# Two block products and a bank copy of an output projection given out ahead of the last gate of the input projection

## The chip, the cores and the metric

One core of a Trainium2 chip runs the kernel. The metric is the device time of one execution in microseconds (us); the median of several runs counts. In the profile, PE is TensorE (matmul), PEld its weight load, DVE is VectorE, ACT is ScalarE, POOL is GpSimd and SP is SyncE, which issues most of the DMAs.

## The reference

One layer of a decoder trunk on a sequence of 1024 tokens and 1024 channels, all in float32:

```
h = rms_norm(x, g_mix)
z = h @ w_in + b_in
va, ga, xb, gb, sa, sb = split(z)            # 1024, 1024, 1536, 1536, 1024, 1024 columns
u   = silu(layer_norm(causal_conv31(va * sigmoid(ga)), ln_g, ln_b))
y_a = u @ w_a_out                            # stage "ga"
v   = rg_lru(causal_conv4(xb))
y_b = (v * gelu(gb)) @ w_b_out               # the stage that is changed
m   = sigmoid(sa) * y_a + sigmoid(sb) * y_b
x   = x + m @ w_o
x   = x + relu(rms_norm(x, g_mlp) @ w_1) ** 2 @ w_2
out = rms_norm(x, g_final)
```

## The kernel before

Every float32 operand is held as two parts in a shorter format, a high part (a ScalarE copy, names ending in `h`) and the low rest (a VectorE subtraction, `l`). A product of two blocks takes three matmuls: high by high, high by low, low by high. Matmuls are 128 x 128 by 128 x 512. Tokens are split into even and odd ones, or into two halves of 512. Larger products are formed from seven products of half blocks instead of eight, with sums of blocks as operands.

The stages follow one another, and TensorE's work is laid out by hand as a list of steps. Two of them matter here:

- **The input projection**, `zseq`. Each step `(i, p)` is one block product of 12 matmuls into a PSUM bank. `z_post` and `z_post2` take the results out one and two steps later: gates go through a sigmoid on ScalarE (tile `zg`, line 937) and are stored to DRAM (`gates`). Two more rounds, `n = L` and `n = L + 1`, follow behind the last step; they take out the last results and prepare operands. The table `ZX` says which loads and splits are given out at which step: `hg_parts(t)` splits tile `t` of the gated recurrence output for the next stage.
- **The product with w_b_out**, `bseq`. For four pairs of output blocks (`i` = 0 to 3), its steps are `"1"` to `"7"` with 6 matmuls each (block products on the four tiles of the recurrence output that go through the seven products, operands `hb1` to `hb7` from `hb_parts` and `hb_t`) and `"00"`, `"01"`, `"10"`, `"11"` with 24 matmuls each (plain products on the other eight tiles, operands `hg0` to `hg9`). `b_mm` gives out the matmuls of a step, `b_post` what follows them at the next step. Results are shared between banks by copies on ScalarE (line 1161): `"1"` is copied from bank b to a, `"7"` from f to an SBUF tile, `"6"` from b to e, `"5"` from e to g. Only then may further matmuls be added to the source bank. The eight banks of PSUM are handed out in turn.

The table `BX` gives the loads and splits for each step of `bseq`: `p_load` and `p_parts` the plain weights (`wbp`), `a_load`, `a_sums` and `a_parts` the weights of the seven products (`wba`, `wbs`), `b_gate` the stored gates (`sb`), `n_load` and `n_ahead` the convolution's output for the layer norm (`q`, `yc`).

Beside these steps runs the layer norm of `u`, a generator `n_all`: statistics of the odd tokens and of the even tokens (`n_stats`: the mean by matmuls with a matrix of ones, eight differences and squares, the variance by matmuls again, a root), then scaling with Silu of the even (`n_scale(0)`) and of the odd tokens (`n_scale(1)`). Where it yields `"pause"`, nothing more of it is given out in this step. `n_to(k)` drives it on until `k` pieces are scaled.

The order on each engine is the order in which this program gives instructions out. What VectorE has to do in a step is first collected by `later` with a time at which it is ready, then sorted by that time in `vector_work`; gaps are filled with pieces of `n_all` according to the planner's own clocks `clk`, which count estimated costs for TensorE, ScalarE and VectorE. ScalarE, VectorE and SP each work through their list in order.

Of the kernel before, what the change touches and what calls it, by code (L numbers as in the profile page):

```python
# [9 lines left out]
F32 = mybir.dt.float32  # L10
# [3 lines left out]
ALU = mybir.AluOpType  # L14
# [16 lines left out]
def trunk_kernel(ctx: ExitStack, tc: tile.TileContext, x, xt_in, xt_eo, vecs, w_in, w_a_out, w_b_pl, w_b_sq,  # L31
# [948 lines left out]
    with tc.manual_schedule(engines=ENGINES):  # L980
# [60 lines left out]
        def p_parts(j):  # L1041
            if j < 8:
                wop[j, "p"] = b_split(wraw_.pop((j, "p")), f"wbp{j}", W if j else T)

        L = len(zseq)
        ZX.update({L - 16: ((a_load, 0),), L - 13: ((a_sums, 0), (hb_load, 0, 0)),
                   L - 12: ((a_parts, 0, "a"), (hb_load, 0, 1)), L - 11: ((a_parts, 0, "s"), (hb_load, 1, 1)),
# [2 lines left out]
                   L - 6: ((hb_parts, 6), (hg_load, 2)), L - 5: ((p_parts, 0), (hg_load, 3, 6)),  # L1050
                   L - 4: ((hg_parts, 0), (hg_load, 7)), L - 3: ((hg_parts, 1), (hg_load, 8)),
                   L - 2: ((hg_parts, 2, 3), (hg_load, 9)), L - 1: ((hb_parts, 2), (hg_parts, 6)),
                   L: ((hg_parts, 7, 8),), L + 1: ((hg_parts, 9),)})
        for n in range(6):
            z_get(n, z_sums)
        vector_work(clk["V"])
# [37 lines left out]
    def W(name, dt=F32):  # L1094
        return wp.tile([P, S], dt, tag="w", name=name)

    def bank(name):
        return zp.tile([P, HS], F32, tag="z", name=name)

    def low(l, src, h):  # L1100
        tt(l, src, h.bitcast(F32), ALU.subtract)  # L1101

    PLAIN = (0, 1, 2, 3, 6, 7, 8, 9)
    bseq = [(0, "1")]
    for i in range(4):
        bseq += [(i, x) for x in ("7", "6", "00", "5", "2", "4", "01", "3", "10")]
        bseq += [(i + 1, "1")] * (i < 3) + [(i, "11")]
    sb, yb_, fs = {}, {}, {}

    def b_gate(j):  # L1110
        for hf in range(2):
            sb[j, hf] = EV(f"sb{j}{hf}").rearrange("p (o n) -> p o n", o=2)
            nc.sync.dma_start(sb[j, hf], halved(spill[1, j], hf))

    def b_mm(i, x):
        if len(x) == 1:
            p = int(x)
            b = {1: "b", 2: "a", 3: "e", 4: "b", 5: "e", 6: "b", 7: "f"}[p]
            if p in (1, 7):
                yb_[i, b] = bank(f"yb{i}{b}")  # L1120
            (h, l), k0 = wop[i, "a" if p in (1, 2, 4) else "s"], \
                {1: 0, 2: 1, 4: 3, 5: 0, 6: 1, 7: 2, 3: 3}[p]
            vh, vl = hbo[p]
            if i == 3:
                del hbo[p]
            ops = [(h[:, c:c + P], l[:, c:c + P], vh[:, hs], vl[:, hs])
                   for c, hs in ((2 * P * k0, HALVES[0]), (2 * P * k0 + P, HALVES[1]))]
            if p in (3, 4):
                del wop[i, "s" if p == 3 else "a"]
            new = p in (1, 7)  # L1130
        else:
            m_, hf = int(x[0]), int(x[1])
            b, new = {"00": "a", "01": "e", "10": "b", "11": "g"}[x], False
            h, l = wop[2 * i + m_, "p"]
            ops = [(h[:, n * P:(n + 1) * P], l[:, n * P:(n + 1) * P], *(a[:, HALVES[hf]] for a in hg[t]))
                   for n, t in enumerate(PLAIN)]
            if hf:
                del wop[2 * i + m_, "p"]
        todo = [y for w, wl, h, l in ops for y in ((w, h), (w, l), (wl, h))]
        for n, (w, v) in enumerate(todo):  # L1140
            nc.tensor.matmul(yb_[i, b], w, v, start=new and n == 0, stop=n == len(todo) - 1,  # L1141
                             skip_group_check=not new)
        at("P", len(todo) * MM)

    def b_out(i, m_, hf, src):
        j = 2 * i + m_
        g = sb.pop((j, hf))

        def mult():
            tt(g, src.rearrange("p (n o) -> p o n", o=2), g, ALU.mult)  # L1150
            nc.sync.dma_start(halved(mbd[j], hf), g)

        later(0, 0.69, mult)

    def b_post(i, x):
        def copy(to, b):
            if to == "f":
                t = fs[i] = EV(f"ybf{i}")
            else:
                t = yb_[i, to] = bank(f"yb{i}{to}")  # L1160
            nc.scalar.activation(t, yb_.pop((i, b)) if to == "f" else yb_[i, b], AF.Copy)
            at("A", 0.62)

        if x in ("1", "7", "6", "5"):
            copy(*{"1": "ab", "7": "ff", "6": "eb", "5": "ge"}[x])
        elif x in ("2", "3"):
            b_out(i, 0, int(x == "3"), yb_.pop((i, "a" if x == "2" else "e")))
        elif x == "10":
            c = EV(f"ybc{i}")
            later(0, 0.69, tt, c, yb_.pop((i, "b")), fs[i], ALU.add)  # L1170
            b_out(i, 1, 0, c)
        elif x == "11":
            c = fs.pop(i)
            later(0, 0.69, tt, c, yb_.pop((i, "g")), c, ALU.add)
            b_out(i, 1, 1, c)


    q, mean, vacc, rstd, nsum, nspl = {}, {}, {}, {}, {}, {}

# [35 lines left out]
    def n_stats(o):  # L1215
        held = []

        def add(s):
            if o in vacc:
                tt(vacc[o], vacc[o], s, ALU.add)  # L1220
                v_at()
            else:
                vacc[o] = s

        n_split(ysum[0][:, HALVES[o]], f"mu{o}")
        yield "pause"
        mean[o] = n_mm(f"mu{o}")
        yield "pause"
        for n, (kk, c2, i) in enumerate(PIECES8):
            if o:  # L1230
                n_ahead(1)
                a = ahead.pop(0)
            else:
                a = q[kk, o, c2][:, HALVES[i]]
            tt(a, a, mean[o], ALU.subtract)
            v_at()
            if o:
                nc.sync.dma_start(yd[4 * kk + 2 * c2 + i, :, HALVES[1]], a)
            s = EV(f"sq{o}{n}")
            nc.scalar.activation(s, a, AF.Square)  # L1240
            at("A", 0.62, clk["V"])
            if held:
                add(held.pop(0))
            held.append(s)
            yield True
        add(held.pop(0))
        mean.pop(o)
        n_split(vacc.pop(o), f"var{o}")
        yield "pause"
        pv = n_mm(f"var{o}")  # L1250
# [25 lines left out]
    def n_all():  # L1276
        yield from n_stats(1)
        while (0, 0, 0) not in q:
            yield "pause"
        yield from n_stats(0)  # L1280
        ysum.clear()
        yield from n_scale(0)
        while (0, 1, 0) not in q:
            yield "pause"
        yield from n_scale(1)

    norm = n_all()

    scaled = [0]
# [466 lines left out]
        7: ((g_parts, "u", 5, 1), (up_lhs, 1, 5), (g_t, "u", 0, 3), (g_t, "u", 1, 3))}.items()})  # L1756
    BX = {}
    for i in range(4):
        BX.update({(i, "7"): ((b_gate, 2 * i), (p_parts, 2 * i + 1), (a_load, i + 1))[::1 if i else 2],
                   (i, "6"): ((p_load, 2 * i + 2),), (i, "5"): ((a_sums, i + 1),),  # L1760
                   (i, "01"): ((a_parts, i + 1, "a"), (b_gate, 2 * i + 1)),
                   (i, "10"): ((a_parts, i + 1, "s"), (p_parts, 2 * i + 2), (p_load, 2 * i + 3))})
    for k, v in {(0, "1"): ((p_load, 1), (hb_parts, 5)), (0, "7"): ((hb_t, 4),), (0, "6"): ((hb_parts, 4),),
                 (0, "00"): ((hb_parts, 3),), (0, "2"): ((p_parts, 1), (n_ahead, 6)), (0, "10"): ((n_load, 0),),
                 (2, "11"): ((n_load, 1),),
                 (3, "00"): ((g_load, "a", 0, 0), (g_load, "a", 1, 0)),
                 (3, "4"): ((n_to, 4), (g_parts, "a", 1, 0), (g_parts, "a", 1, 1)),
                 (3, "01"): ((g_load, "a", 2, 0), (g_load, "a", 3, 0), (g_get, 0, g_lhs), (g_get, 1, g_lhs)),
                 (3, "3"): ((n_to, 16), (g_t, "a", 0, 1, 2), (g_t, "a", 1, 1, 2), (g_get, 2, g_lhs),
                           (g_get, 3, g_lhs)),  # L1770
                 (3, "10"): ((g_load, "a", 0, 1),),
                 (3, "11"): ((g_parts, "a", 2, 0), (g_parts, "a", 2, 1), (g_load, "a", 1, 1))}.items():
# [413 lines left out]
```

## Time and profile before

| | |
|---|---|
| time, median of 3 runs | 1552.56 us (1552.04 to 1553.2) |
| the profiled execution: its own time | 1549.72 us |
| its span | 1548.0 us |
| granted TensorE clock, mean over the span | 0.998 |
| first matmul of `bseq` | 628.72 us from the span's start |
| first matmul of `ga`, the stage behind it | 765.78 us |

In the profile, a row of a timeline has the start in us from the span's start, the duration, the engine, the line, the operation and `written<-read`. In brackets behind it stands how long the engine had been idle just before it, and what released it. A row of the windows has the stretch, its length and the busy time of PE, PEld, DVE, ACT and POOL with instruction counts, then the granted TensorE clock, the DMA share and GB/s.

### The profile page before, as it was taken

How to read it: one execution, taken by the hardware profiler on the slowest of the kernel's cores; microseconds unless marked ns; L12 is line 12 of the kernel's file. 1: busy time of each engine (PE TensorE's matmuls, PEld its weight loads, DVE VectorE, ACT ScalarE, POOL GpSimd, SP SyncE). 2: the span in 40 equal slices, each digit the busy share in tenths (PEclk: the TensorE clock that was granted, in tenths of full speed). 3: DMA queues.
4: the chain of work that ended last, by engine and by line, in shares of the span. 5: the costliest groups of instructions: out<-in, count | busy, mean ns of one | idle time of the engine just before them, and what ended most of it. 6: DMA issues, size and time to landing. Idle time of an engine off the chain costs nothing.

```text
span 1548.0 us, 19213 instructions
## 1 busy us (share of the span) xinstructions
PE 1530.0 (99%) x6758; PEld 1258.2 (81%) x6758; DVE 1247.2 (81%) x1679; ACT 917.4 (59%) x1280; POOL 184.4 (12%) x219
## 2 busy tenths in 40 slices
PE   9999999999999999899999999999999999999998
PEld 7888788888888888788788888888888888888886
DVE  6899999979899998687779879755555558888897
ACT  6648576567667567544575777554444475555553
POOL 0000000002222222000022332000000001111110
PEclk9999999999999999999999999999999999999999
DMA  8776978898997779863779898333333779888862
GB/s 345 196 188 161 250 189 223 217 275 219 251 245 200 184 193 275 271 205 116 240 210 300 195 195 214 137 121 113 114 115 110 242 210 228 220 224 223 209 129 109
DMA packets 134593, 312.03 MB, mean 202 GB/s; under 512 B 13488, under 2 KB 35504, under 8 KB 134496
## 3 DMA queue, kind: packets, MB, share of 16 engines
q1 hardware_dynamic: 104048, 234.79, 46.7%
q0 software_dynamic: 30304, 75.74, 26.7%
q8 instruction: 53, 0.87, 0.2%
q14 instruction: 44, 0.36, 0.1%
q10 hardware_dynamic: 144, 0.26, 0.0%
HBM read 149.79 MB, written 60.82 MB: 136 GB/s over the span
## 4 chain that ended last, share of the span: by engine, by line
PE 89%; issue 4%; DMA 2%; DVE 1%; POOL 1%; ACT 1%; SPq 0%; POOLq 0%; ACTq 0%; DVEq 0%
PE z L726 18%; PE d L1948 15%; PE e L2068 3%; PE keep L1948 2%; PE z L258 1%; PE rg L536 1%; PE rg L534 1%; PE rg L535 1%; DMA x<-in_x_dram 1%; PE yb0b L1141 1%; ACT q L1270 1%; POOL go L66 1%; PE yb3e L1141 1%; PE yb1b L1141 1%; PE yb0e L1141 1%
## 5 line engine op out<-in xcount | busy, mean ns | idle before, releaser
L726 PE MATMUL z<-xh,win_h 128*128 128x512 f32 x400 | 125.0, 391 | 0.0
L726 PE MATMUL z<-xl,win_h 128*128 128x512 f32 x400 | 124.6, 390 | 0.0
L1960 DVE TENSOR_TENSOR acc<-acc,d 128x1024 f32<-128x1024 f32 x72 | 87.9, 1220 | 33.4 <-PE d L1948 32.7
L726 PE MATMUL z<-xh,win_l 128*128 128x512 f32 x400 | 98.3, 391 | 0.0
L726 PEld LDWEIGHTS z<-xh,win_l 128*128 128x128 f32 x400 | 75.2, 188 | 16.8
L726 PEld LDWEIGHTS z<-xh,win_h 128*128 128x128 f32 x400 | 75.0, 188 | 16.7 <-ACT win_h L67 0.7
L637 DVE SCALAR_TENSOR_TENSOR y<-u,vec,y 128x511 f32<-128x511 f32 (+14 forms) x120 | 88.5, 738 | 0.0
L726 PEld LDWEIGHTS z<-xl,win_h 128*128 128x128 f32 x400 | 75.1, 188 | 15.8
L542 ACT ACTIVATE g<-rg,vec 96x1024 f32<-96x1024 f32 x32 | 35.6, 1113 | 85.1 <-issue 46.0
L637 DVE SCALAR_TENSOR_TENSOR y<-yt,csum,y 128x511 f32<-128x511 f32 (+6 forms) x112 | 82.7, 738 | 0.0
L637 DVE SCALAR_TENSOR_TENSOR yt<-u,vec,yt 128x511 f32<-128x511 f32 (+6 forms) x112 | 82.7, 738 | 0.0
L1645 ACT ACTIVATE o<-s 128x512 fp32r<-128x512 f32 x56 | 33.7, 622 | 45.6 <-DVE s L1629 26.4
L66 POOL DMA_DIRECT2D win_l<-win_raw x25 | 21.8, 871 | 324.6 <-ACT win_l L65 294.8
L66 POOL DMA_DIRECT2D zo<-zw x42 | 36.6, 871 | 128.2 <-ACT zo L65 116.6
L486 DVE SCALAR_TENSOR_TENSOR v<-xb,vec,v 128x1023 f32<-128x1023 f32 (+2 forms) x36 | 46.2, 1283 | 7.0 <-ACT v L477 6.0
L66 POOL DMA_DIRECT2D db_1l<-wr x7 | 6.1, 869 | 310.2 <-ACT db_1l L65 287.6
L65 ACT ACTIVATE zo<-zw 128x512 fp32r<-128x512 f32 x42 | 26.3, 626 | 20.8 <-PE z10f L914 2.1
L1101 DVE TENSOR_TENSOR o<-s,o 128x512 fp32r<-128x512 f32 x56 | 37.3, 683 | 1.5 <-ACT o L1645 1.4
L66 POOL DMA_DIRECT2D zo<-zs x28 | 24.5, 873 | 76.2 <-ACT zo L65 70.9
L578 DVE TENSOR_TENSOR_SCAN g<-a,g 128x1024 f32<-128x1024 f32 x12 | 27.5, 2292 | 0.4
L66 POOL DMA_DIRECT2D ga<-gsa x8 | 7.0, 871 | 170.4 <-ACT ga L65 168.3
L67 ACT ACTIVATE win_h<-win_raw 128x1024 fp32r<-128x1024 f32 x25 | 26.2, 1046 | 0.0
(2825 smaller groups left out, 4854.2 us busy)
## 6 DMA issues: line engine op xcount, KB each, us to landing
w_raw<-in_w_dram SPq DMA_DIRECT2D x34, 512.0 KB, 5.4
fr<-fd SPq DMA_DIRECT2D x32, 512.0 KB, 5.3
wr<-in_w_dram SPq DMA_DIRECT2D x32, 512.0 KB, 6.1
zw<-in_w_in_dram SPq DMA_DIRECT2D x28, 512.0 KB, 5.6
win_raw<-in_w_in_dram SPq DMA_DIRECT2D x25, 512.0 KB, 7.0
win_l<-win_raw POOLq DMA_DIRECT2D x25, 512.0 KB, 6.6
zo<-zw POOLq DMA_DIRECT2D x42, 256.0 KB, 5.7
gates<-zg SPq DMA_DIRECT2D x32, 256.0 KB, 4.0
```

The source lines that it names most:

```text
L66: nc.gpsimd.dma_start(l, src, accum_op=ALU.add)
L486: nc.vector.scalar_tensor_tensor(v[:, d:S], a[:, 0:S - d], cbw_c[:, w * 12 + t:w * 12 + t + 1], v[:, d:S], ALU.mult, ALU.add)
L542: nc.scalar.activation(a, gps.pop((n, gi))[:HD, :], AF.Sigmoid, bias=(ba_c, bx_c)[gi][:, n:n + 1])
L578: nc.vector.tensor_tensor_scan(i, a, i, 0.0, ALU.mult, ALU.add)
L637: nc.vector.scalar_tensor_tensor(o[:, k:], a[:, 0:HS - k], c, o[:, k:], ALU.mult, add)
L726: nc.tensor.matmul(zps[s][:, HALVES[hf]], w[:, k, :], xw[k][part][hf], start=n == 0, stop=n == 23)
L1101: tt(l, src, h.bitcast(F32), ALU.subtract)
L1141: nc.tensor.matmul(yb_[i, b], w, v, start=new and n == 0, stop=n == len(todo) - 1, skip_group_check=not new)
L1645: nc.scalar.activation(o[:, 0], src, AF.Copy)
L1948: nc.tensor.matmul(o, a, b, start=n == 0 and (p != 1 or g == 0), stop=n == len(todo) - 1, skip_group_check=p == 1 and g > 0)
L1960: tt(acc[p, q2], acc[p, q2], ps, ALU.add)
L2068: nc.tensor.matmul(o, a, b, start=n == 0 and t not in LOADED, stop=n == len(todo) - 1, skip_group_check=t in LOADED)
```

## The change

- The helpers `bank`, `b_gate`, `b_mm`, `b_out` and `b_post` move ahead of the loop of the input projection, unchanged but for two calls spelled out.
- In round `L`, behind hg7, the steps (0,"1") and (0,"7") of `bseq` are given out. In round `L + 1` the copy of (0,"1") from bank b to bank a is given out ahead of the last gate's sigmoid; hg8 moves from round `L` to `L + 1`, hg9 to step (0,"6"). The loop over `bseq` starts with its third step, (0,"6").
- `BX` of the first steps: the first load of plain weights (`p_load` 1), the first gates (`b_gate` 0), `a_load` 1, hg9, hb5 and `hb_t` 4 all belong to (0,"6") now; hb4 to (0,"00") and hb3 to (0,"5"), one step later each.
- `n_stats` pauses once more between the split of a sum (mean and variance) and its matmuls.
- `n_scale(1)`, the odd tokens, starts at step (3,"5") instead of as soon as their load has been given out.

```diff
@@ ahead of the loop of the input projection: bank, bseq, b_gate, b_mm, b_out, b_post moved here @@
-                   L: ((hg_parts, 7, 8),), L + 1: ((hg_parts, 9),)})
+                   L: ((hg_parts, 7), (b_mm, 0, "1"), (b_mm, 0, "7")),
+                   L + 1: ((b_post, 0, "1"), (hg_parts, 8))})
...
@@ n_stats @@
         n_split(ysum[0][:, HALVES[o]], f"mu{o}")
         yield "pause"
+        yield "pause"
         mean[o] = n_mm(f"mu{o}")
...
         n_split(vacc.pop(o), f"var{o}")
         yield "pause"
+        yield "pause"
         pv = n_mm(f"var{o}")
...
@@ n_all @@
         yield from n_scale(0)
-        while (0, 1, 0) not in q:
+        while not landed:
             yield "pause"
         yield from n_scale(1)
 
+    landed = []
...
     for i in range(4):
-        BX.update({(i, "7"): ((b_gate, 2 * i), (p_parts, 2 * i + 1), (a_load, i + 1))[::1 if i else 2],
+        BX.update({(i, "7"): ((b_gate, 2 * i), (p_parts, 2 * i + 1), (a_load, i + 1)),
...
-    for k, v in {(0, "1"): ((p_load, 1), (hb_parts, 5)), (0, "7"): ((hb_t, 4),), (0, "6"): ((hb_parts, 4),),
-                 (0, "00"): ((hb_parts, 3),), (0, "2"): ((p_parts, 1), (n_ahead, 6)), (0, "10"): ((n_load, 0),),
+    BX[0, "6"] = (p_load, 1), (b_gate, 0), (a_load, 1), (hg_parts, 9), (hb_parts, 5), (hb_t, 4), (p_load, 2)
+    for k, v in {(0, "00"): ((hb_parts, 4),), (0, "5"): ((hb_parts, 3),), (0, "2"): ((p_parts, 1), (n_ahead, 6)),
+                 (0, "10"): ((n_load, 0),),
                  (2, "11"): ((n_load, 1),),
...
-                 (3, "4"): ((n_to, 4), (g_parts, "a", 1, 0), (g_parts, "a", 1, 1)),
+                 (3, "5"): ((landed.append, 1),), (3, "4"): ((n_to, 4), (g_parts, "a", 1, 0), (g_parts, "a", 1, 1)),
...
-        for n, step in enumerate(bseq):
+        for n, step in enumerate(bseq[2:], 2):
             taps["paused"] = False
             clk["A"], clk["V"] = max(clk["A"], clk["P"] + 0.5), max(clk["V"], clk["P"] - 2)
-            if n:
-                b_post(*bseq[n - 1])
+            b_post(*bseq[n - 1])
             b_mm(*step)
```

More of the change, by code (lines that the diff above doesn't have):

```diff
@@ L1043, in p_parts, with bank, b_gate @@
                 wop[j, "p"] = b_split(wraw_.pop((j, "p")), f"wbp{j}", W if j else T)
+        def bank(name):
+            return zp.tile([P, HS], F32, tag="z", name=name)
+        PLAIN = (0, 1, 2, 3, 6, 7, 8, 9)
+        bseq = [(0, "1")]
+        for i in range(4):
+            bseq += [(i, x) for x in ("7", "6", "00", "5", "2", "4", "01", "3", "10")]
+            bseq += [(i + 1, "1")] * (i < 3) + [(i, "11")]
+        sb, yb_, fs = {}, {}, {}
+        def b_gate(j):
+            for hf in range(2):
+                sb[j, hf] = EV(f"sb{j}{hf}").rearrange("p (o n) -> p o n", o=2)
+                nc.sync.dma_start(sb[j, hf], halved(spill[1, j], hf))
@@ new lines, in b_mm @@
+        def b_mm(i, x):
+            if len(x) == 1:
+                p = int(x)
+                b = {1: "b", 2: "a", 3: "e", 4: "b", 5: "e", 6: "b", 7: "f"}[p]
+                if p in (1, 7):
+                    yb_[i, b] = bank(f"yb{i}{b}")
+                (h, l), k0 = wop[i, "a" if p in (1, 2, 4) else "s"], \
+                    {1: 0, 2: 1, 4: 3, 5: 0, 6: 1, 7: 2, 3: 3}[p]
+                vh, vl = hbo[p]
+                if i == 3:
+                    del hbo[p]
+                ops = [(h[:, c:c + P], l[:, c:c + P], vh[:, hs], vl[:, hs])
+                       for c, hs in ((2 * P * k0, HALVES[0]), (2 * P * k0 + P, HALVES[1]))]
+                if p in (3, 4):
+                    del wop[i, "s" if p == 3 else "a"]
+                new = p in (1, 7)
+            else:
+                m_, hf = int(x[0]), int(x[1])
+                b, new = {"00": "a", "01": "e", "10": "b", "11": "g"}[x], False
+                h, l = wop[2 * i + m_, "p"]
+                ops = [(h[:, n * P:(n + 1) * P], l[:, n * P:(n + 1) * P], *(a[:, HALVES[hf]] for a in hg[t]))
+                       for n, t in enumerate(PLAIN)]
+                if hf:
+                    del wop[2 * i + m_, "p"]
+            todo = [y for w, wl, h, l in ops for y in ((w, h), (w, l), (wl, h))]
+            for n, (w, v) in enumerate(todo):
+                nc.tensor.matmul(yb_[i, b], w, v, start=new and n == 0, stop=n == len(todo) - 1,
+                                 skip_group_check=not new)
+            at("P", len(todo) * MM)
@@ new lines, in b_out, with mult, b_post, copy @@
+        def b_out(i, m_, hf, src):
+            j = 2 * i + m_
+            g = sb.pop((j, hf))
+            def mult():
+                nc.vector.tensor_tensor(g, src.rearrange("p (n o) -> p o n", o=2), g, ALU.mult)
+                nc.sync.dma_start(halved(mbd[j], hf), g)
+            later(0, 0.69, mult)
+        def b_post(i, x):
+            def copy(to, b):
+                if to == "f":
+                    t = fs[i] = EV(f"ybf{i}")
+                else:
+                    t = yb_[i, to] = bank(f"yb{i}{to}")
+                nc.scalar.activation(t, yb_.pop((i, b)) if to == "f" else yb_[i, b], AF.Copy)
+                at("A", 0.62)
+            if x in ("1", "7", "6", "5"):
+                copy(*{"1": "ab", "7": "ff", "6": "eb", "5": "ge"}[x])
+            elif x in ("2", "3"):
+                b_out(i, 0, int(x == "3"), yb_.pop((i, "a" if x == "2" else "e")))
+            elif x == "10":
+                c = EV(f"ybc{i}")
+                later(0, 0.69, nc.vector.tensor_tensor, c, yb_.pop((i, "b")), fs[i], ALU.add)
+                b_out(i, 1, 0, c)
+            elif x == "11":
+                c = fs.pop(i)
+                later(0, 0.69, nc.vector.tensor_tensor, c, yb_.pop((i, "g")), c, ALU.add)
+                b_out(i, 1, 1, c)
@@ L1095, in W @@
         return wp.tile([P, S], dt, tag="w", name=name)
-    def bank(name):
-        return zp.tile([P, HS], F32, tag="z", name=name)
     def low(l, src, h):
         tt(l, src, h.bitcast(F32), ALU.subtract)
[L1103 to L1175, printed above, removed]
```

## The prediction

> **What bounds the kernel now.** I read the page first, then the waits of TensorE, then the timelines of the stage that the change touches, engine by engine.
>
> ```profile
> PE 1530.0 (99%) x6758; PEld 1258.2 (81%) x6758; DVE 1247.2 (81%) x1679; ACT 917.4 (59%) x1280; POOL 184.4 (12%) x219
> ```
>
> TensorE is busy for 1530.0 of 1548.0 us, so no other engine's busy time is worth anything by itself; only TensorE's idle time can be won. The change takes no matmul away. The waits of TensorE between 625 and 960 us:
>
> ```profile
> PE yb0b L1141 <- ACT yb0a L1161: 4.5, 1, 4.5
> PE yb3e L1141 <- ACT yb3e L1161: 2.3, 1, 2.3
> PE mu L1202 <- DVE mu0l L1101: 0.8, 1, 0.8
> ```
>
> (Columns: sum, times, longest.) These three are all, and each lies in the stage of `bseq`. The question is whether the edits meet them, and what comes late next.
>
> The first one, in TensorE's timeline (start, duration), and the granted clock (after the counts) in the 4 us behind it:
>
> ```profile
> 628.72 0.39 PE L1141 MATMUL yb0b<-hb1h,wba0h 128*128 128x512 f32 x1
> ...
> 629.86 0.39 PE L1141 MATMUL yb0b<-hb1h,wba0l 128*128 128x512 f32 x1
> ...
> 631.22 0.39 PE L1141 MATMUL yb0f<-hb7h,wbs0l 128*128 128x512 f32 x1
> 636.07 0.50 PE L1141 MATMUL yb0b<-hb6h,wbs0h 128*128 128x512 f32 x1 [4.46 <-ACT yb0a L1161]
> ...
> 644.61 0.39 PE L1141 MATMUL yb0e<-hb5h,wbs0h 128*128 128x512 f32 x1
> ```
>
> ```profile
> 636.00:640.00 4.00, 3.93 (x11) 3.12 (x12) 2.82 (x3) 2.51 (x5) 0.00 (x0) 0.61 0.86 248
> ```
>
> Steps (0,"1") and (0,"7") run, then (0,"6") may not write bank yb0b until ScalarE has copied it. From 628.72 to 631.22 eleven matmuls start one behind the other: 2.50 / 11 = 0.227 us each. The 42 matmuls of (0,"1"), (0,"7"), (0,"6") and (0,"00") should therefore take 9.54 us; they take 644.61 - 628.72 = 15.89. The loss is 6.35 us: 4.62 of standing still (636.07 - 631.22 - 0.227), and 1.73 because the clock came back at 0.61. Why the copy is late stands in ScalarE's timeline:
>
> ```profile
> 629.13 1.05 ACT L991 ACTIVATE hg7h<-hg 128x1024 fp32r<-128x1024 f32 x1
> 630.08 1.05 ACT L991 ACTIVATE hg8h<-hg 128x1024 fp32r<-128x1024 f32 x1
> 632.88 1.06 ACT L991 ACTIVATE hg9h<-hg 128x1024 fp32r<-128x1024 f32 x1 [1.75 <-DMA hg<-hgd]
> 633.85 0.74 ACT L937 ACTIVATE zg<-zu,vec 128x512 f32<-128x512 f32 x1
> 634.50 1.04 ACT L991 ACTIVATE hb5h<-hb 128x1024 fp32r<-128x1024 f32 x1
> 635.44 0.57 ACT L1161 ACTIVATE yb0a<-yb0b 128x512 f32<-128x512 f32 x1
> ```
>
> Its source is complete at 629.86 + 0.39 = 630.25, but it stands behind hg9h, which waits for a load, and behind the sigmoid and hb5h.
>
> **Part 1: two block products and the copy given out early; hg9 later.** In the new order ScalarE has hg7h, the copy, hg8h, the sigmoid, the copy of yb0f, hg9h, hb5h, the copy to yb0e. The copy starts when its source is complete, at about 630.3, and ends at 630.9; (0,"6") can start at 631.22 + 0.227 = 631.45. So the wait goes, with 0.5 us to spare, and the cold clock with it: 6.35 us.
>
> What is late next? Continuing at 0.227 us: (0,"00") from 632.81, (0,"5") 638.26, (0,"2") 639.6, (0,"4") 641.0, (0,"01") 642.3, (0,"3") 647.8, (0,"10") 649.2. Three things moved later or into another order, with these rows for the prices:
>
> ```profile
> 633.97 1.23 DVE L462 TENSOR_TENSOR hg9l<-hg,hg9h 128x1024 fp32r<-128x1024 f32 x1 [0.42 <-ACT hg9h L991]
> ```
>
> ```profile
> 634.62 0.51 SPq L939 DMA_DIRECT2D gates<-zg  x1
> 635.23 1.24 SPq L1113 DMA_DIRECT2D sb<-gates  x2
> 636.63 0.48 SPq L1020 DMA_DIRECT2D wba<-in_w_b_sq_dram  x1
> ```
>
> ```profile
> 642.76 0.43 DVE L462 TENSOR_TENSOR wbs<-wba 128x256 f32<-128x256 f32 x1 [0.97 <-DMA wba<-in_w_b_sq_dram]
> ```
>
> (a) hg9 is the last operand of (0,"00"), from its 22nd matmul on, 632.81 + 21 x 0.227 = 637.6. Its load lands at 632.88. ScalarE reaches hg9h after hg8h (about 630.9 + 1.0), the sigmoid (0.7) and a copy (0.57): 633.0, so the load is just hidden, and hg9h ends at 634.1. VectorE does the difference of `hb_t` 4 first (it is ready at once; 1.23, to 634.7), then hg9l to 635.9: 1.7 us of cover. hb5l follows to 637.1, for 638.3; hb4 is given out one step later and its low half ends at about 638.3, for 641.0. (b) The last sigmoid now ends at 632.5, 2.1 us earlier, and SP's queue behind it starts as much earlier: gate store, load of wbp1 (before, ahead of the store), two sb loads, wba1, wbp2. wba1 leaves at about 632.5 + 2.0 (634.62 to 636.63) + 0.6 for wbp1 = 635.1 and lands, at the 6.13 us of the row (636.63 to 642.76), at 641.2. (c) hb3 now sits in step (0,"5") with `a_sums` 1, and the list is sorted by readiness: the four sums (ready 0) stand ahead of hb3's low half and wait for wba1. VectorE: sums to 642.9 (4 x 0.43 at most), hb3l to 644.2, wbp1l to 645.4. Needed at 647.8 and 649.2: 3.6 us of cover on each. I take nothing for (a) to (c).
>
> **Part 2: one more pause in front of each mean and variance matmul.** The stall that it meets:
>
> ```profile
> 688.16 0.69 DVE L1101 TENSOR_TENSOR mu0l<-ysum,mu0h 128x512 fp32r<-128x512 f32 x1
> ```
>
> ```profile
> 687.73 0.40 PE L1201 MATMUL mu<-mu0h,onesm 128*128 128x512 f32 x1
> 688.90 0.51 PE L1202 MATMUL mu<-mu0l,onesm 128*128 128x512 f32 x1 [0.78 <-DVE mu0l L1101]
> ...
> 694.74 0.39 PE L1141 MATMUL yb2b<-hb1h,wba2h 128*128 128x512 f32 x1
> ```
>
> From 687.73 to 694.74 there are 26 matmuls, 5.90 us at 0.227; it takes 7.01. Loss 1.1 us. With the pause, mu0's matmuls follow (1,"10") instead of (1,"3"): 24 matmuls or 5.45 us later, against 0.9 us that were wanted. Gain 1.1. The price is that the chain of the norm loses four steps in all. Counting with the planner's own costs (0.69 a vector piece, 0.62 a scalar one, 3.8 the root), mu of the odd tokens is split in (0,"01") as before, its differences start in (1,"1"), the even tokens' mean is split in (1,"01"), their root comes in (2,"01"), and the last even scaling in (2,"11") instead of (2,"10"). The four that (3,"4") demands are done with (2,"3"), so nothing is forced out ahead of time.
>
> **Part 3: odd tokens scaled from (3,"5") on.** The stall, on VectorE, ScalarE and TensorE, and the load behind it:
>
> ```profile
> 731.06 4.15 SPq L1185 DMA_DIRECT2D q<-yd  x8
> ```
>
> ```profile
> 735.36 5.57 DVE L1268 TENSOR_TENSOR q<-q,lr 128x512 f32<-128x512 f32 x8 [4.97 <-DMA q<-yd]
> ```
>
> ```profile
> 736.09 5.84 ACT L1270 ACTIVATE q<-q,vec 128x512 f32<-128x512 f32 x8 [5.70 <-DVE q L1268]
> ...
> 743.26 0.58 ACT L1161 ACTIVATE yb3e<-yb3b 128x512 f32<-128x512 f32 x1
> ```
>
> ```profile
> 741.24 0.39 PE L1141 MATMUL yb3a<-hg9h,wbp6l 128*128 128x512 f32 x1
> 743.89 0.50 PE L1141 MATMUL yb3e<-hb5h,wbs3h 128*128 128x512 f32 x1 [2.27 <-ACT yb3e L1161]
> ...
> 745.38 0.39 PE L1141 MATMUL yb3a<-hb2h,wba3h 128*128 128x512 f32 x1
> ```
>
> Eight Silus, waiting for a load asked for only at 731.06, stand ahead of the copy to yb3e that (3,"5") needs. Loss: 743.89 - 741.24 - 0.227 = 2.42, and 745.38 - 743.89 - 6 x 0.227 = 0.13; together 2.55. In the new order this copy stands ahead of the Silus. The next copy that TensorE needs is yb3g<-yb3e, before (3,"01") writes yb3e again; four Silus (4 x 0.73 = 2.9 us) stand ahead of it. The load leaves in the same step, and (2,"11"), (3,"7"), (3,"6") and (3,"00") are 13.6 us of matmuls; it began to land 4.3 us after its issue and took 4.15 us to issue, so the eight are there about 9 us after the first issue. Silus and copy are done during (3,"5") and (3,"2"), and (3,"4") is spare. Behind that ScalarE has 5.45 us of (3,"01") and as much of (3,"10") for the rest. Gain 2.55, no new price.
>
> **Sum.** 6.35 + 1.1 + 2.55 = 10.0 us. On the profiled execution's own time, 1549.7 (span 1548.0 and 1.7 around it), that gives 1539.7; the median of the runs lies 2.9 above that execution, and I carry the difference over: 1552.56 - 10.0 = 1542.5.
>
> A rule to weigh: behind 4.46 us of idle TensorE the clock was 0.61, behind 2.27 us the second matmul already took 0.40. [...]
>
> **The rivals.** *A train of loads.* wbp1, two sb, wba1 and wbp2 now leave one behind the other where wbp1 had left alone before the stall. If wba1 takes 12 us instead of 6.13, it lands at 647.1, the sums end at 648.8 and hb3l at 650.0 against 647.8: TensorE waits 2.2 us, 1544.7. Against it: VectorE waited only 0.97 for wba1 with two sb loads ahead of it. Chance 0.12. *One of the smaller stalls stays,* 1.1 or 2.55 us, or both, since the chain of the norm is one planned with estimated costs: 1543.6 to 1546.2. Chance 0.12. *The copy is early but (0,"6") waits all the same,* because what it waits on is not the copy alone (a bank's earlier reader, since yb0f and yb0a change places in the turn of eight banks): Part 1 is lost, 1548.9, or with a further wait no change. For it: nothing; (0,"7") and the copy found their banks free. Chance 0.04. *The chain comes too late, and the time is longer.* The point is (3,"4"): if the differences of the even tokens are not out by then, `n_to` gives them out in one go, and TensorE's variance matmuls stand behind them ahead of (3,"01"). Eight differences and eight sums at 0.70 (5.57 / 8) are 11.1 us of VectorE, 1.7 for the cold clock, and root, sixteen scalings and the operands of the next stage overrun the remaining 17.7 us of matmuls by some 4: 17 us lost against 10 won, 1559.5. It decides if the even tokens' mean comes out as late as (3,"00"); my count puts it sixteen steps earlier, in (1,"10"). For it: four steps are given away, and the planner's clocks are not the chip's. Chance 0.05.
>
> **How the numbers follow.** The forecast, all three stalls gone, has 0.67; with 1 us of unseen small things on each side it covers 1541 to 1544. With the first two rivals, to 1546.8, it reaches 0.9; I take 1540.8 to 1546.8 since prices add. A measurement tells 0.2% (3.1 us) from no change here. Faster by more: forecast, first two rivals and half of the third, 0.93; no change 0.02; slower 0.05.
>
> **What would show it.** Right: no wait of yb0b on yb0a, TensorE's clock at 1.00 in the 12 us behind (0,"7"), the copy yb0a ahead of hg8h on ScalarE, no wait at mu0, and the Silus of the odd tokens behind the copy to yb3e; `ga` starts 10 us earlier. Wrong in a step: a wait of (0,"00") on hg9l, of (0,"3") on hb3l, of (3,"01") on yb3g. The whole is wrong if TensorE's waits in this stage again add up to over 5 us.

## The result and the profile after

The changed kernel takes 1539.23 us (median of 6 runs, 1538.92 to 1540.03), the kernel before, run beside it, 1552.27 (6 runs, 1549.65 to 1553.2): a ratio of 0.9918, 95% interval 0.9906 to 0.9931. The gain is 13.0 us. The forecast was a gain of 10.0, to 1542.5, with a range from 1540.8 to 1546.8; the measured time lies below it.

The profiled execution of after took 1539.30 (span 1537.5 and 1.8 around it), that of before 1549.72: 10.4 us between the two. The page's busy line of after:

```profile
PE 1527.8 (99%) x6758; PEld 1256.9 (82%) x6758; DVE 1246.3 (81%) x1679; ACT 917.8 (60%) x1280; POOL 184.4 (12%) x219
```

The stage of `bseq`, from its first matmul to the first one of `ga`, in one window each (before, then after; the columns are length, then busy time and instructions of PE, PEld, DVE, ACT and POOL, the granted clock, the DMA share and GB/s):

```profile
628.70:765.80 137.10, 129.59 (x562) 106.09 (x561) 100.80 (x131) 63.86 (x87) 0.00 (x0) 0.99 0.59 194
```

```profile
628.50:755.50 127.00, 127.00 (x561) 105.13 (x560) 100.00 (x131) 63.71 (x87) 0.00 (x0) 1.00 0.63 209
```

127.00 of 127.00 us, at a mean clock of 1.00: in after TensorE never stands still in this stage and never runs slowly. The stage is 10.1 us shorter. What this stage takes beyond 127.0 us is called its *loss* below: time in which TensorE stood still or ran slowly.

TensorE's waits of after between 625 and 960 us, all of them:

```profile
PE gu1a L1384 <- DMA gu<-w_raw: 0.7, 1, 0.7
```

None of the three waits of before is left. (This one lies at 916 us, far behind the stage; three of four further profiled executions of before have it too, with 0.7, 0.3 and 0.2.) The places of the three, in TensorE's timeline:

```profile
631.00 0.39 PE L1086 MATMUL yb0f<-hb7h,wbs0l 128*128 128x512 f32 x1
631.23 0.39 PE L1086 MATMUL yb0b<-hb6h,wbs0h 128*128 128x512 f32 x1
...
686.58 0.39 PE L1201 MATMUL mu<-mu0h,onesm 128*128 128x512 f32 x1
686.81 0.39 PE L1202 MATMUL mu<-mu0l,onesm 128*128 128x512 f32 x1
...
733.56 0.39 PE L1086 MATMUL yb3a<-hg9h,wbp6l 128*128 128x512 f32 x1
733.78 0.39 PE L1086 MATMUL yb3e<-hb5h,wbs3h 128*128 128x512 f32 x1
```

Each of the three pairs is 0.22 or 0.23 apart, one matmul behind the other.

### The profile page after: what moved, and what is told of

It reads as the page before. It is cut to its first block, busy times and chain, and to the rows that moved or that the text cites. A ratio compares the mean times of both kernels' runs of the same rounds, so it can differ in the third digit from the quotient of the medians.

```text
span 1537.5 us, 19209 instructions
## 1 busy us (share of the span) xinstructions
PE 1527.8 (99%) x6758; PEld 1256.9 (82%) x6758; DVE 1246.3 (81%) x1679; ACT 917.8 (60%) x1280; POOL 184.4 (12%) x219
## 4 chain that ended last, share of the span: by engine, by line
PE 95%; DMA 2%; issue 1%; DVE 1%; SPq 0%; POOL 0%; ACT 0%; POOLq 0%; DVEq 0%
PE z L726 18%; PE d L1951 15%; PE e L2071 3%; PE keep L1951 2%; PE z L258 1%; PE rg L534 1%; PE rg L536 1%; PE rg L535 1%; DMA x<-in_x_dram 1%; PE yb2b L1086 1%; PE yb1b L1086 1%; PE yb3b L1086 1%; PE yb0b L1086 1%; DMA gu<-w_raw 1%; PE yb3e L1086 1%
## 5 line engine op out<-in xcount | busy, mean ns | idle before, releaser
L65 ACT ACTIVATE win_l<-win_raw 128x1024 fp32r<-128x1024 f32 x25 | 26.2, 1046 | 0.0
```

Source lines behind the costliest of these rows:

```text
L65: nc.scalar.activation(l, src, AF.Copy, scale=-1.0)
```

## Experiments: each part alone

Parts 1, 2 and 3 were each tried alone on the kernel before, and the kernel before was run once more. Beside them the kernel before took 1552.9 us (median of 21 runs). A gain is given as the difference of the medians; "by the interval" means the 95% interval of the ratio, turned into us. Theories A to C, which some expectations name, are set out with the repeat of the kernel before, below.

**Part 1 alone**: the changed kernel without the pauses and with the old start of the odd tokens.

```diff
@@ after.py, n_stats, twice @@
         yield "pause"
-        yield "pause"
@@ n_all @@
-        while not landed:
+        while (0, 1, 0) not in q:
             yield "pause"
```

> Part 1 alone: the first two block products, the copy and the loads as in the change; one pause only in n_stats and odd tokens scaled as before. In the profile I expect no wait of yb0b, the waits of mu0 and yb3e still there: span about 1541.6. Times, against 1552.3: theory A 9.2 us less (1543.1), theories B and C 6.35 less (1546).

Measured: 1548.24 (1546.3 to 1550.85), ratio 0.9959 (0.9946 to 0.9973). The first stall is gone. The gain is 4.7 by the medians and 4.2 to 8.4 by the interval, so it can't be told from 6.35; the 9.2 of theory A lies outside. The profiled execution was the slowest of the five (1550.85), and in it a part of the gain is lost again at mu0:

```profile
682.75 0.40 PE L1201 MATMUL mu<-mu0h,onesm 128*128 128x512 f32 x1
685.15 0.67 PE L1202 MATMUL mu<-mu0l,onesm 128*128 128x512 f32 x1 [2.00 <-DVE mu0l L1176]
685.62 0.63 PE L1086 MATMUL yb1b<-hg0h,wbp3h 128*128 128x512 f32 x1
686.04 0.63 PE L1086 MATMUL yb1b<-hg0l,wbp3h 128*128 128x512 f32 x1
```

TensorE came to mu0 5.0 us earlier than in before (682.75 for 687.73). VectorE's chain of the root, which ends in mu0l, came only 3.75 us earlier (684.41 for 688.16). The wait grew from 0.78 to 2.00, and behind it matmuls start 0.43 us apart instead of 0.227. Taking one stall away may lengthen the next. This execution alone doesn't show it, since two of the five executions of before, further down, wait 1.6 and 2.0 here too; the runs without the pauses, below, do.

**Part 2 alone**: the two pauses on the kernel before.

```diff
@@ before.py, n_stats, twice @@
         yield "pause"
+        yield "pause"
```

> Part 2 alone: one more pause before each mean and variance matmul, all else as before. My count: the wait of 0.8 us at mu0 goes, 1.1 us less by all theories, 1551.2; the yb0b and yb3e waits stay.

Measured: 1552.26, ratio 0.9992 (0.9983 to 1.0001), not told from no change, nor from the forecast 1.1: the interval is from 0.2 us lost to 2.6 won. The wait at mu0 is gone in its profile. But the next one, at yb3e, is 3.0 us there and is followed by slow matmuls. The window from 744 us on:

```profile
744.00:748.00 4.00, 3.66 (x9) 2.89 (x10) 0.00 (x0) 0.98 (x3) 0.00 (x0) 0.50 0.78 257
```

Nine matmuls in it, at a clock of 0.50. The execution that the prediction was made on lost 0.13 to slow running behind this wait, this one 2.9.

**Part 3 alone**: the odd tokens from (3,"5") on, on the kernel before.

```diff
@@ before.py, n_all @@
-        while (0, 1, 0) not in q:
+        while not landed:
             yield "pause"
...
+    landed = []
@@ BX @@
+                 (3, "5"): ((landed.append, 1),),
```

> Part 3 alone: odd tokens scaled from (3,"5") on, all else as before. The wait at yb3e goes, those of yb0b and mu0 stay. Theories A and C: 2.55 us less, 1549.7. Theory B: 5.4 less, 1546.9.

Measured: 1547.59 (1547.29 to 1548.49), ratio 0.9961 (0.9949 to 0.9974): 5.3 us by the medians, 4.0 to 7.9 by the interval: as theory B had it (5.4), and twice the 2.55 of my sum. In its profile the wait at yb3e is gone, those at yb0b (4.5) and mu0 (0.9) stand as before.

**The kernel before once more**, with no edit:

> The kernel before, once more, with a second profile. The question: five of its six runs took 1552.0 to 1553.2 us, one 1549.65 and the profiled one 1549.7, while the changed kernel's all lie within 1538.9 to 1540.0. Theory A (the long executions have a longer TensorE stall at the bank copy of (0,"1"), with the clock cold for longer than the 1.73 us of the profile): if the second profile is a long one (span about 1550.5), the extra 2.5 to 3 us lie between the starts of yb0b and yb0e of pair 0, 18.4 us or more instead of 15.9. Theory B: they lie at the wait for the copy to yb3e, 5 us or more there instead of 2.4. Theory C: they lie outside the stage of bseq. If the profile is again a short one, it says nothing on this.

Measured: 1551.98 (11 runs), ratio 0.9994. Its profiled execution took 1551.29, 1.6 more than the one I had predicted from. VectorE's scalings of the odd tokens and TensorE's third stall in it:

```profile
735.74 0.69 DVE L1268 TENSOR_TENSOR q<-q,lr 128x512 f32<-128x512 f32 x1 [4.55 <-DMA q<-yd]
737.65 4.74 DVE L1268 TENSOR_TENSOR q<-q,lr 128x512 f32<-128x512 f32 x7 [1.22 <-DMA q<-yd]
```

```profile
745.42 0.50 PE L1141 MATMUL yb3e<-hb5h,wbs3h 128*128 128x512 f32 x1 [2.99 <-ACT yb3e L1161]
745.75 0.40 PE L1141 MATMUL yb3e<-hb5l,wbs3h 128*128 128x512 f32 x1
```

The load came in two instalments, with a second wait of 1.22 for it, and the wait at yb3e was 2.99 for 2.27. So the stalls are not of one size. That gave the question for the rest: are the 2.9 us between the profiled execution and the median *in the stalls*, so that they went with them?

## Experiments: useless matmuls in the stalls

These kernels are the kernel before with additional matmuls into a spare bank, whose result nobody reads. They are there to keep TensorE busy during a wait. If standing still is what makes TensorE run slowly behind a wait, the slow running should go.

```diff
@@ before.py, the loop over bseq, behind b_mm(*step) @@
+            if step in FILL:
+                spare_ = bank(f"fill{step[0]}")
+                for _ in range(FILL[step]):
+                    nc.tensor.matmul(spare_, onesm, hg[0][0][:, 0:HS], start=True, stop=True)
@@ warm @@
+    FILL = {(0, "7"): 18, (3, "00"): 10}
@@ warm3 @@
+    FILL = {(3, "00"): 10}
@@ warm1 @@
+    FILL = {(0, "7"): 18}
```

> The kernel before with the waits left as they are, but TensorE kept busy in two of them: 18 matmuls with no use (into a spare bank, 18 x 0.227 = 4.1 us) behind (0,"7") and 10 (2.3 us) behind (3,"00"). The copies still end when they end. Theory A (what the other executions lose beyond the profiled one is cold clock behind these two waits, plus a longer wait at yb3e): no matmul at 0.43 us behind either wait, and the time falls by all the cold parts, 1.7 to 2.6 us at the first and up to 2.8 at the second: 1548 to 1549.5. Theory C (a constant part outside the stage): 1552.6 - 1.7 - 0.1 = 1550.8, no less.

Measured: 1548.03 (1547.12 to 1550.7), ratio 0.9975 (0.9967 to 0.9984): 3.8 us won by useless work. In its profile TensorE stands idle for 0.2 us at yb0b and 0.5 at yb3e, for 4.5 and 2.3 in before. The useful matmuls still wait for the same copies, so what was won should be slow running and not standing still. Behind the first wait only the next matmul starts late, after 0.33 us:

```profile
633.79 1.76 PE L1786 MATMUL fill<-hg0h,onesm 128*128 128x512 f32 x7
635.78 0.50 PE L1141 MATMUL yb0b<-hb6h,wbs0h 128*128 128x512 f32 x1 [0.22 <-ACT yb0a L1161]
636.11 0.39 PE L1141 MATMUL yb0b<-hb6l,wbs0h 128*128 128x512 f32 x1
```

In the execution that the prediction was made on, slow running cost 1.9 us in all (1.73, and 0.1 at each of the other two). 3.8 (2.5 to 5.1 by the interval) is more: the usual execution seems to lose more to it than the one I read.

> The kernel before with 10 useless matmuls (2.3 us) behind (3,"00") alone; the first wait is left idle. warm, with both filled, was 3.8 us faster than before. Theory A (cold clock behind both): the first one costs 1.7 to 2.6 us of cold clock, so this run is 1.2 to 2.1 us faster than before, 1550 to 1550.6. If all the variable part is at the yb3e wait: 3 us faster or more, 1549.

Measured: 1551.5 (1551.01 to 1552.43), ratio 0.9999 (0.999 to 1.0007): nothing, against what I expected. Filling the third stall alone is worth nothing that these runs can tell. In its profile the wait at yb3e is down to 0.4 as intended, but the unfilled one at yb0b is 5.4, longer than in any profiled execution of before; why, no run shows.

> The kernel before, with 18 useless matmuls behind (0,"7") alone (0.227 us each, 4.1 us: they fill most of TensorE's first wait and keep it busy). Theory first stall (what the median of the kernel before has beyond its profiled execution lies behind yb0b's wait, as a colder clock): the two sets of useless matmuls together brought 3.8 us, those behind (3,"00") alone nothing, so these bring all of it, 3.8: a ratio of 0.9975, 1548 us where the kernel before takes 1551.9. Theory third stall (it lies at yb3e's wait, whose length depends on the load): these bring only the 1.7 us of cold clock that the profiled execution had there, a ratio of 0.9989, about 1550.2.

Measured: 1550.0 (1547.66 to 1552.83), ratio 0.9987 (0.9978 to 0.9996): 2.2 us by the medians, 0.6 to 3.4 by the interval. The 3.8 expected if the first stall held everything lies outside it. In its profile the wait at yb0b is down to 0.7, and it is behind the third stall, after a wait of 2.76, that TensorE goes slow, from the fourth matmul on:

```profile
744.01 0.50 PE L1141 MATMUL yb3e<-hb5h,wbs3h 128*128 128x512 f32 x1 [2.76 <-ACT yb3e L1161]
...
744.58 0.40 PE L1141 MATMUL yb3e<-hb5h,wbs3l 128*128 128x512 f32 x1
744.81 0.56 PE L1141 MATMUL yb3e<-hb5h,wbs3h 128*128 128x512 f32 x1
745.17 0.63 PE L1141 MATMUL yb3e<-hb5l,wbs3h 128*128 128x512 f32 x1
```

So neither place holds it alone. Three more profiled executions of the kernel before, unchanged, show why.

> The kernel before unchanged, one more profiled execution, to see where its time above 1549.7 us lies. Theory first stall: with a time of 1551.5 to 1553, the stage from (0,"7") to (0,"3") loses 7.5 to 9 us instead of 6.35, its matmuls behind the wait standing at 0.43 us for longer. Theory third stall: the first stage loses 6.3 as before, and yb3e's wait is 3 to 4 us instead of 2.3, with slow matmuls behind it. A time near 1549.7 goes with 6.35 and 2.55 by both.

> The same kernel and the same two readings as in the look before this one.

> The same kernel and the same two readings as in the two looks before this one.

The window of the stage in the first repeat and in these three (second to fourth repeat), each with its own start and end:

```profile
628.80:767.30 138.50, 130.61 (x562) 106.87 (x561) 100.72 (x131) 63.91 (x87) 0.00 (x0) 0.98 0.58 191
```

```profile
628.80:766.30 137.50, 129.57 (x561) 106.04 (x561) 100.60 (x131) 63.91 (x87) 0.00 (x0) 0.99 0.59 193
```

```profile
628.80:768.00 139.20, 130.87 (x562) 106.98 (x562) 100.56 (x131) 63.98 (x87) 0.00 (x0) 0.98 0.58 192
```

```profile
628.50:770.00 141.50, 131.87 (x562) 107.70 (x562) 100.72 (x131) 64.05 (x87) 0.00 (x0) 0.96 0.57 188
```

The loss is the window less 127.0. By stall it is worked out from the starts of the matmuls, each distance less 0.227, and written as standing still + running slowly:

| execution of before | own time | loss | own time less loss | at yb0b | at mu0 | at yb3e |
|---|---|---|---|---|---|---|
| the one predicted from | 1549.72 | 10.1 | 1539.6 | 4.6 + 1.7 | 0.95 + 0.1 | 2.4 + 0.1 |
| second repeat | 1551.01 | 10.5 | 1540.5 | 4.6 + 1.7 | 0.95 + 0.1 | 2.8 + 0.1 |
| first repeat | 1551.29 | 11.5 | 1539.8 | 4.3 + 2.7 | 0.94 + 0.1 | 3.15 + 0.1 |
| third repeat | 1552.08 | 12.2 | 1539.9 | 4.4 + 2.9 | 1.7 + 0.1 | 2.7 + 0.1 |
| fourth repeat | 1553.85 | 14.5 | 1539.4 | 5.2 + 2.3 | 2.15 + 1.7 | 2.8 + 0.1 |

The own times spread over 4.1 us; less the loss of this stage, over 1.1. The changed kernel, with no loss, takes 1539.3. So nearly all of the spread of the kernel before is the three stalls, and the execution I read was the one with the smallest. (In the profiled executions of the other kernels here, the own time less the loss is 1538.3 to 1541.2, but for part 1 alone with 1542.2, whose stage begins 1.4 us later than before's: a microsecond or two can lie outside the stalls.) The extra sits in a different stall each time: slow running behind yb0b and a longer wait at yb3e in the first repeat, slow running behind yb0b and a longer wait at mu0 in the third, a longer wait at mu0 in the fourth, where slow matmuls follow as well:

```profile
691.11 0.50 PE L1202 MATMUL mu<-mu0l,onesm 128*128 128x512 f32 x1 [1.98 <-DVE mu0l L1101]
...
692.38 0.61 PE L1141 MATMUL yb1b<-hg1l,wbp3h 128*128 128x512 f32 x1
692.78 0.63 PE L1141 MATMUL yb1b<-hg1h,wbp3l 128*128 128x512 f32 x1
```

Where a longer wait could be followed back, it goes to a load that landed later: that of q at yb3e (above), and at mu0 that of wba2, whose sums stand on VectorE ahead of the root. In the fourth repeat sums and root began 2.4 and 2.2 us later than in the execution predicted from (676.68 and 681.12 there), while TensorE came to mu0 only 1.0 us later:

```profile
679.13 0.42 DVE L462 TENSOR_TENSOR wbs<-wba 128x256 f32<-128x256 f32 x1 [2.48 <-DMA wba<-in_w_b_sq_dram]
...
683.33 3.35 DVE L98 RECIPROCAL lr<-lsd 128x512 f32<-128x512 f32 x1 [1.44 <-ACT lsd L1254]
```

This load was not slower, it was asked for later. From its issue to the first sum it took 5.85 us, for 5.95 in the execution predicted from. SP issued it at 673.28, for 670.73, because it stands in SP's queue behind four stores of yc, and the last of these follows VectorE's last difference (670.86, for 668.31). Why the differences came later stays open.

## Experiments: the change less one part

**Without the pauses** (part 1 and 3):

```diff
@@ after.py, n_stats, twice @@
         yield "pause"
-        yield "pause"
```

> The changed kernel without part 2 (one pause only in n_stats). In part 1 alone the wait at mu0 was 2.0 us instead of 0.8 and the clock went cold behind it. If part 1 makes mu0's wait longer, the pauses are worth more with it than alone: a wait at mu0 of about 2 us, 2 to 4 us over the changed kernel, 1541.3 to 1543.5. If the stalls are independent (part 2 worth 0.6 to 1.1 us as measured alone): 1539.9 to 1540.4.

Measured: 1543.97 (1541.84 to 1545.16), ratio 0.9948 (0.9934 to 0.9961).

```profile
683.59 0.50 PE L1202 MATMUL mu<-mu0l,onesm 128*128 128x512 f32 x1 [1.91 <-DVE mu0l L1176]
```

The wait at mu0, 0.78 in before, is back with 1.91, as in part 1 alone. The profiled execution was the fastest of the five (1541.84), and no slow matmul follows the wait there. What the others lost beyond it is in no trace; slow running of 1.7 us as in part 1 alone would be most of what the median lost besides.

**Without part 1**: the diffs of part 2 alone and part 3 alone, both on the kernel before.

> The changed kernel without part 1: the kernel before with the pauses and the later scaling. If the parts add up as measured alone (0.6 and 5.3 us): 1552.6 - 5.9 = 1546.7, and part 1 is worth 7.5 us here, of which the profile should show 4.5 us of waiting at yb0b and the rest as matmuls at 0.43 us. If part 1 were worth only what it gained alone (4.7), this would be at 1544.

Measured: 1546.37 (1545.88 to 1546.77), ratio 0.9962 (0.9949 to 0.9974). The wait at yb0b is 5.0 us in its profile, the other two are gone.

**Without part 3**: the old start of the odd tokens in the changed kernel.

```diff
@@ after.py, n_all @@
-        while not landed:
+        while (0, 1, 0) not in q:
             yield "pause"
```

> The changed kernel without part 3: odd tokens scaled as soon as their load has been given out. The wait at yb3e is back: 2.3 to 3.1 us, with or without cold clock behind it (up to 2.8 us). From part 3 alone (5.3 us): 1544.5. From the profiled execution (2.55 us): 1541.8.

Measured: 1544.43 (1544.13 to 1544.98), ratio 0.9953 (0.9941 to 0.9965). The wait at yb3e is 3.26 us in its profile, with slow matmuls behind it.

What each part is worth in us, by the medians (alone: against 1552.9, with the interval; as the last one: from the kernel without it to 1539.23, across sets of runs beside which the kernel before took 1551.8 to 1552.3):

| part | forecast | alone | as the last one |
|---|---|---|---|
| 1, early block products and copy | 6.35 | 4.7 (4.2 to 8.4) | 7.1 |
| 2, pauses | 1.1 | 0.6 (-0.2 to 2.6) | 4.7 |
| 3, odd tokens later | 2.55 | 5.3 (4.0 to 7.9) | 5.2 |

Part 2 differs most: not told from nothing by itself, 4.7 us beside the other two, once part 1 has brought TensorE early to mu0. All five runs without it took 1541.84 us or more, all six of the changed kernel 1540.03 or less.

## Experiments: how late may the copy be?

The prediction's reason for part 1 is the place of the copy on ScalarE. Three kernels were to move it back there.

```diff
@@ after.py, round L + 1 @@
-                   L + 1: ((b_post, 0, "1"), (hg_parts, 8))})
+                   L + 1: ((hg_parts, 8),)})
@@ copylate: first pass of the loop over bseq @@
+            if n == 2:
+                b_post(0, "1")
@@ copylate2 and copylast instead: in round L + 1, behind the last gate's sigmoid @@
             z_get(n - 2, z_post2)
+            if n == L + 1:
+                b_post(0, "1")
@@ copylast besides: hg9 from (0,"6") back to round L + 1 @@
+                   L + 1: ((hg_parts, 8, 9),)})
```

> The changed kernel with one thing undone: the copy from yb0b to yb0a stands behind hg8h and the last sigmoid again (hg9 and hb5 stay behind it). On ScalarE it then ends at about 632.7 instead of 630.6, and (0,"6"), due at 631.2, waits 1.5 us. If the place of the copy on ScalarE is what made the first stall: a wait of yb0b on yb0a of 1.5 us and 1540.7 (1.5 us over the changed kernel), up to 1543 where the clock goes cold behind so short a wait. If early products by themselves were what mattered: no change, 1539.2.

Measured: 1539.1, ratio 0.9915 (0.9902 to 0.9929), no change, but this tests nothing: ScalarE's timeline has the copy ahead of hg8h as in the changed kernel. The edit moved the copy from one block of fixed order (`manual_schedule`, the input projection's) into the next (that of `bseq`), and it still came out ahead of what the first block gives out last. So across two such blocks an engine's order need not be the order of giving out.

```profile
630.16 0.58 ACT L1106 ACTIVATE yb0a<-yb0b 128x512 f32<-128x512 f32 x1
631.00 1.06 ACT L991 ACTIVATE hg8h<-hg 128x1024 fp32r<-128x1024 f32 x1 [0.25 <-DMA hg<-hgd]
```

> The changed kernel with the copy yb0a<-yb0b given out behind the last gate's sigmoid, in the same round, so that on ScalarE it stands behind hg8h and the sigmoid (in copylate it had kept its place ahead of hg8h). It should end at about 632.8; (0,"6"), due at 631.2 to 631.4, waits about 1.4 us. If the copy's place in ScalarE's list makes the first stall: a wait of yb0b on yb0a of 1.4 us, 1540.7, and up to 1542.5 where the clock goes cold behind it. If the early products alone matter: no wait, 1539.2.

Measured: 1540.13, ratio 0.9926 (0.9912 to 0.9939), 0.9 above the changed kernel; its profiled execution loses 1.0 in the stage. Here the copy is given out inside the first block. It stands behind hg8h and the sigmoid, at 631.99, and TensorE waits for it. Only the first matmul behind the wait is slow:

```profile
632.61 0.50 PE L1086 MATMUL yb0b<-hb6h,wbs0h 128*128 128x512 f32 x1 [0.70 <-ACT yb0a L1106]
632.95 0.39 PE L1086 MATMUL yb0b<-hb6l,wbs0h 128*128 128x512 f32 x1
```

> As copylate2, and hg9 split in round L + 1 again, so that the copy stands behind hg8h, hg9h (which waits for its load, landing at about 633) and the sigmoid, but still ahead of hb5h. It should end at about 635.1; (0,"6") waits 3.7 us. By the place of the copy: a wait of 3.7 us, 1543 with a warm clock, 1544.5 to 1545.5 with a cold one. Rival: hg9 is wanted early and the wait is made up for later in (0,"00"): under 1541.

Measured: 1545.58 (1544.73 to 1546.13), ratio 0.996 (0.9947 to 0.9972), 6.35 above. Behind hg9h, which waits for its load, the copy starts at 634.56; TensorE waits 3.97 us, and in the window from 635 to 639 nine matmuls run at a clock of 0.50:

```profile
635.20 0.80 PE L1086 MATMUL yb0b<-hb6h,wbs0h 128*128 128x512 f32 x1 [3.97 <-ACT yb0a L1106]
```

```profile
635.00:639.00 4.00, 3.80 (x9) 3.06 (x10) 2.63 (x3) 2.44 (x5) 0.00 (x0) 0.50 0.75 209
```

So the first term is shown at its own place. With hg9's split and the copy behind it, and everything else as in the changed kernel, the whole first stall is back: 4.1 us of standing still and 2.65 of slow running by the starts of the matmuls. (That the times differ by the forecast 6.35 to the digit is chance; this profiled execution loses 6.9 in the stage.)

## Why the prediction was right or wrong

**The sum was right for the execution it was made on.** 10.0 us from 1549.7, to 1539.7; the profiled execution of after took 1539.30 and its stage was 10.1 shorter. All three stalls went, and no new one came.

**The step that failed** is the last one: "the median of the runs lies 2.9 above that execution, and I carry the difference over". I treated the 2.9 as something of the runs that a change leaves alone. The five executions show that what lies above the one I read is the same three stalls, larger (10.5 to 14.5 us of loss, for 10.1); with the stalls it went too. The forecast would have been 1539.7 by the sum alone, against 1539.23. The range failed with it: its lower end, 1540.8, stood above the sum's own answer, so that the case "the difference goes as well" had no place in it.

**The terms as medians** do not add up, since the stalls act on one another. Alone the parts bring 4.7 + 0.6 + 5.3 = 10.6, as the last one 7.1 + 4.7 + 5.2 = 17.0, and together 13.0. Part 3 was too small in both, 2.55 against 5.3 and 5.2. At its place the five executions of before lost 2.5 to 3.3, the one without part 3 lost 5.1 (3.43 + 1.7), and the one of part 2 alone 6.1. That explains its worth as the last one. Alone, 5.3 is more than before loses there in any execution I have. At the other two stalls the execution of part 3 alone lost 7.5, like the two lowest of the five; the other three lost 8.2 to 11.5 there. Whether part 3 has a hand in that, or the runs fell so, stays open.

**Part 1, step by step.** ScalarE in after:

```profile
628.85 1.05 ACT L991 ACTIVATE hg7h<-hg 128x1024 fp32r<-128x1024 f32 x1
630.06 0.58 ACT L1106 ACTIVATE yb0a<-yb0b 128x512 f32<-128x512 f32 x1 [0.17 <-PE yb0b L1086]
630.56 1.05 ACT L991 ACTIVATE hg8h<-hg 128x1024 fp32r<-128x1024 f32 x1
631.51 0.75 ACT L937 ACTIVATE zg<-zu,vec 128x512 f32<-128x512 f32 x1
632.16 0.58 ACT L1106 ACTIVATE ybf<-yb0f 128x512 f32<-128x512 f32 x1
632.97 1.06 ACT L991 ACTIVATE hg9h<-hg 128x1024 fp32r<-128x1024 f32 x1 [0.23 <-DMA hg<-hgd]
```

The order is the one forecast. The copy ends at 630.64 (forecast 630.9) and (0,"6") starts at 631.23 (631.45). hg9h starts at 632.97; the forecast's sum for it, 630.9 + 1.0 + 0.7 + 0.57, is 633.2 and not the 633.0 written there. Slow running was not in proportion to the wait: 1.73 us behind 4.46 in before, 2.65 behind copylast's 3.97, 0.1 behind copylate2's 0.70.

The covers (a) and (c), on VectorE:

```profile
634.31 1.22 DVE L462 TENSOR_TENSOR hg9l<-hg,hg9h 128x1024 fp32r<-128x1024 f32 x1
635.45 1.22 DVE L462 TENSOR_TENSOR hb5l<-hb,hb5h 128x1024 fp32r<-128x1024 f32 x1
...
640.49 0.43 DVE L462 TENSOR_TENSOR wbs<-wba 128x256 f32<-128x256 f32 x1 [2.69 <-DMA wba<-in_w_b_sq_dram]
...
641.97 1.22 DVE L462 TENSOR_TENSOR hb3l<-hb,hb3h 128x1024 fp32r<-128x1024 f32 x1
```

(a) hg9l ends at 635.5 (forecast 635.9), hb5l at 636.7 (637.1): each ahead of its matmul. (c) The sums wait for wba1 as forecast and hb3l ends at 643.2 (644.2), needed at 647.6: the train of loads stayed a rival that did not happen.

(b) SP's queue was read wrongly, without cost:

```profile
627.70 0.55 SPq L1039 DMA_DIRECT2D wbp<-in_w_b_pl_dram  x1
632.29 0.51 SPq L939 DMA_DIRECT2D gates<-zg  x1
...
634.31 0.47 SPq L1020 DMA_DIRECT2D wba<-in_w_b_sq_dram  x1
```

The load of wbp1 did not move behind the gate store; it left at 627.70, and wba1 0.8 us sooner than I had it, at 634.31.

**Part 2.** mu0's two matmuls follow (1,"10"), 0.23 apart, as forecast. The pauses cost nothing: no later wait appears in the stage.

**Part 3.** ScalarE in after:

```profile
728.54 0.58 ACT L1106 ACTIVATE yb3e<-yb3b 128x512 f32<-128x512 f32 x1 [0.76 <-PE yb3b L1086]
729.04 2.93 ACT L1272 ACTIVATE q<-q,vec 128x512 f32<-128x512 f32 x4
735.34 0.58 ACT L1106 ACTIVATE yb3g<-yb3e 128x512 f32<-128x512 f32 x1 [3.38 <-PE yb3e L1086]
```

The copy to yb3e stands ahead of the odd tokens' Silus and ends 4.7 us before (3,"5") starts, at 733.78. Four Silus follow and end at 731.97. The copy to yb3g then waits 3.38 us for its own source, so the Silus cost nothing.

**The other rivals** did not happen: no smaller stall stayed, (0,"6") did not wait at all, and the chain of the norm was in time.

## What to carry to other kernels

A profiled execution is one draw: where the time before spreads over several us, ask whether the spread lies in the very stalls that the change removes, and if it may, let the range reach to the sum taken from the profiled execution's own time. Stalls in a row are not separate terms: one that goes brings TensorE sooner to the next, so a small edit that can't be told from nothing alone (part 2) can be worth 4.7 us beside others. And where an early copy is the point, moving it back step by step on its engine (0.9, then 6.4 us lost) tells more than taking the whole edit out, if the timeline shows that it did move.

## What the runs showed of the hardware

Whether TensorE runs slowly behind a stop in this stage did not depend on the stop's length alone. By the starts of the matmuls, behind up to 1.7 us of standing still only the one matmul behind the stop was late (0.34 us to the next start, for 0.227). Behind 4.1 us and more, ten stops in ten profiled executions, matmuls always started 0.43 us apart for a while, and 1.6 to 2.9 us were lost. Between 2.1 and 3.4 us it went both ways, six slow of twelve: at mu0 2.17 us (part 1 alone) and 2.15 (fourth repeat) were followed by slow matmuls, 2.08 (without the pauses) were not; at yb3e 3.15 (first repeat) were not, 2.92 (behind the first stall filled alone) were. What else decides it, no run shows. The fourth repeat's stop of 2.15 us cost 3.85 in all (2.15 + 1.7).
